# A hybrid attention and convolution layer: the convolution's state outputs written by DMA with exchanged dimensions instead of transposed on TensorE

## The chip, the cores and the metric

The kernel runs on one core of one Trainium2 chip. The metric is the device time of one execution in microseconds (us). The kernel before took 470.9 us, the median of three runs (470.34 to 470.97).

## The reference

One layer of a streaming encoder for two requests that share the weights: a prompt of 1024 frames and a running stream of 64 frames, both of model width 1024, with 16 meta tokens. One input projection gives q, k, v, an attention gate, a GLU pair and a convolution gate. Group A is sliding-window attention, group B a depthwise convolution of width 31; both are normalised, gated and go through a shared output projection.

```
a, b = jnp.split(glu, 2, axis=-1)
u = a * jax.nn.sigmoid(b)
...
conv = _conv_branch(u, left, conv_w, ln_g, ln_b, w_pw)
...
new_conv_prompt = u[:, -(CONV_W - 1):]                                   # (30, 512)
new_conv_sample = concatenate([state_conv, us], axis=1)[:, -(CONV_W-1):] # (30, 512)
```

The last two lines, shortened here, are the outputs that the change touches: the last 30 rows of the convolution's input, for the prompt and for the running stream, with 512 channels in a row.

## The kernel before

All 1104 tokens go through the input projection feature-major: a weight tile of 128 output features (`w_in[m]`, 128 x 1024, loaded into `wraw`) is split into two float32r parts, `whi` and `wlo`, and three products, hi·hi, hi·lo and lo·hi, make up a float32 product on TensorE. `unit(mi, n, done)` gives the 24 products of weight tile `mi` and token chunk `n` (384, 384 and 336 or 320 tokens) as a list of closures; `fill(k)` runs the next k of them from a queue, `drain()` all that are left, so the order of TensorE's work is written out by hand. `WORDER` is the order of the weight tiles: 20 is the keys, 21 the values, 4 to 7 and 8 to 11 the GLU pair, 0 to 3 the queries, 12 to 19 the gates.

`ahead` runs the weights' pipeline. In the first unit of a tile it issues the load of the tile after next (`load_raw`, line 184, on SyncE's queue, two `wraw` buffers). In a later unit it splits the next tile: `whi` on ScalarE, and `wlo` on VectorE or by a copy of -whi on ScalarE and an accumulating DMA of `wraw` from GpSimd's queue. For the GLU tiles, `wlo` is made half by the one and half by the other. A `wraw` buffer is free for the next load when both are done.

The GLU units write `u{i}` for i = 0 to 3: 128 channels on the partitions, and along the row 30 state columns, 1024 prompt columns, 30 state columns and 64 sample columns (`UW` in all). Its last piece is written by VectorE in `glu`, after which the 31 taps of the convolution over `u{i}` (`conv`) go on a list. VectorE works through the taps between its other duties: `tick` issues taps as long as the time given to VectorE is less than that given to TensorE plus `AHEAD`, counted in the table `given` by fixed prices. `mm` and `tp` add the prices of TensorE's work.

`conv_outs(i)` writes the state outputs of 128 channels. The columns `SEQ` to `SEQ + LEFT` of `u{i}` are the last 30 prompt frames, the last 30 columns those of the running stream. Both are transposed on TensorE into one PSUM tile (`uo{i}`, line 108), copied by ScalarE into `uso{i}`, and written by two DMAs of 30 rows x 512 B (lines 479 and 480). Its four calls stand among the units: for u0 after the first key unit, for u1 in the middle of the last key unit, for u2 in the last value unit and for u3 in the last unit of the first query tile.

Matmuls, ScalarE, VectorE and GpSimd instructions keep the order in which the program gives them. SyncE's DMAs in this stage are placed by the tile framework's scheduler, which knows what each of them waits for, and stay in that order on the queue.

Of the kernel before, what the change touches and what calls it, by code (L numbers as in the profile page):

```python
# [10 lines left out]
F32 = mybir.dt.float32  # L11
F32R = mybir.dt.float32r
AF = mybir.ActivationFunctionType
ALU = mybir.AluOpType

P = 128
D = 1024
SEQ = 1024
# [8 lines left out]
LEFT = W - 1  # L27
UW = LEFT + SEQ + LEFT + DEC
# [20 lines left out]
def layer_kernel(ctx: ExitStack, tc: tile.TileContext, x, x_fm, w_in, w_pw, w_out, vec, g_post,  # L49
                 bias_in, cache_kT, cache_k, cache_v, stateT,  # L50
                 y_p, y_s, nk_p, nv_p, nc_p, nk_s, nv_s, nc_s):
    nc = tc.nc
# [40 lines left out]
    act, dve, pool = Engine(nc.scalar, "act", 200, 0.82), Engine(nc.vector, "dve", 60, 1.18), Engine(nc.gpsimd)  # L93
# [12 lines left out]
    def tp(*a, **k):  # L106
        given["pe"] += 109
        return tc.keep_in_program_order(nc.tensor.transpose(*a, **k))  # L108
# [5 lines left out]
    sm = ctx.enter_context(tc.tile_pool(name="sm", bufs=2))  # L114
    psum = ctx.enter_context(tc.tile_pool(name="psum", bufs=1, space=bass.MemoryType.PSUM))

    def ps_tile(tag, bufs, name):
        return psum.tile([P, 512], F32, tag=tag, bufs=bufs, name=name)
# [14 lines left out]
    def any_ps(i, name):  # L133
        return ps_tile(*(("mm", 3), ("s", 2), ("pt", 2))[i % 3], name)

    def slot(tag, name, shape=(P, 1152), dt=F32):
        return m4.tile(list(shape), dt, tag=tag, bufs=4 if tag == "B" else 2, name=name)
# [3 lines left out]
    ident = const.tile([P, P], F32, name="ident")  # L141
# [329 lines left out]

    def conv_outs(i):
        u = us[i]
        ps = ps_tile("pt", 2, f"uo{i}")
        tp(ps[:LEFT, 0:P], u[:, SEQ:SEQ + LEFT], ident)
        tp(ps[:LEFT, P:2 * P], u[:, UW - LEFT:UW], ident)
        so = sm.tile([P, 2 * P], F32, tag="gate", bufs=7, name=f"uso{i}")
        act.activation(so[:LEFT], ps[:LEFT, :2 * P], AF.Copy)
        nc.sync.dma_start(nc_p[:, i * P:(i + 1) * P], so[:LEFT, 0:P])
        nc.sync.dma_start(nc_s[:, i * P:(i + 1) * P], so[:LEFT, P:2 * P])  # L480

    def conv(i):
        u = us[i]
# [420 lines left out]
    add_kv(KM, kTb)  # L904
    fill(24)
    conv_outs(0)
    fill(36)
    conv_outs(1)
    drain()
    add_ab(2)  # L910
    drain()
    vfm = slot("T", "vfm")
    add_kv(VM, vfm)
    fill(60)
    conv_outs(2)
    drain()
    add_ab(3)
    fill(24)
    kxy = split_keys()
    for g in range(3):  # L920
        ps = ps_tile("pt", 2, f"vt{g}")
# [13 lines left out]
    so = slot("P", "kvo", (P, 2 * P))  # L935
# [22 lines left out]
    i = -1  # L958
    while (i := i + 1) < max(len(order) + 2, L0 + 7 if L0 < 99 else 0):
# [9 lines left out]
        if 3 <= i < len(order) + 3:  # L969
            c = order[i - 3]  # L970
# [18 lines left out]
        if n == 0:  # L989
            while taps:  # L990
                f, j = taps.pop(0)
# [138 lines left out]
    for T in (0, 1, 8, 2, 3, 4, 5, 6, 7):  # L1130
# [12 lines left out]
        for j, (j0, j1) in enumerate(zip(cuts, cuts[1:])):  # L1143
            js = slice(j0, j1)
            for half in (1, 0):
                ps = any_ps(ny := ny + 1, f"y{T}_{j}_{half}")[:, :j1 - j0]
# [23 lines left out]
        o = slot("P", f"o{T}", (P, D))  # L1170
# [79 lines left out]
```

## Time and profile before

| | |
|---|---|
| median of three runs | 470.9 us (470.34 to 470.97) |
| the profiled execution | 470.69 us |
| its span in the profile | 468.9 us |
| granted clock of TensorE, mean over the span | 0.997 |
| TensorE busy (matmul) | 456.2 us, 97% |
| VectorE busy | 380.1 us, 81% |
| ScalarE busy | 231.3 us, 49% |
| GpSimd busy | 75.0 us, 16% |
| packets on SyncE's DMA queue | 14584, 37.31 MB |

The profiled execution lies 0.2 us below the median of the runs, and 1.8 us of its time are outside the span. PE is TensorE, PEld its weight loads, DVE VectorE, ACT ScalarE, POOL GpSimd; SPq and POOLq are the sequencers of SyncE and GpSimd, which issue DMAs. In the profile most operations of ScalarE, VectorE and GpSimd have line 86, where a helper records them, and all matmuls line 104, so they are told apart by their tiles; the profile leaves the numbers of tiles out (`u` for `u0`, `out_dram` for every output). The input projections before the attention reach from the start to about 187 us; the four calls of `conv_outs` lie at 64, 70, 106 and 144 us.

### The profile page before, as it was taken

Reading aid. Unit: us, or ns where it says so; the run is one execution under the profiler, and the core shown is the slowest. Engines: PE = TensorE matmul, PEld = TensorE weight load, DVE = VectorE, ACT = ScalarE, POOL = GpSimd, SP = SyncE. Lnnn points to the kernel's source line nnn. Section 1 sums busy time; section 2 is a strip of 40 time slices with the busy share of each in tenths; the row PEclk is TensorE's granted clock in tenths of the full one; section 3 lists DMA queues with packets and bytes.
Section 4 is the critical chain, followed back from the end, with each engine's and each line's share of the span. In section 5 each row is a group of like instructions: output and inputs, shape, how many; then the busy total and the mean of one; then the engine's idle time right before and its main releaser. Section 6 shows DMA issues by size and latency. Waiting matters only on the chain.

```text
span 468.9 us, 7427 instructions
## 1 busy us (share of the span) xinstructions
PE 456.2 (97%) x2809; PEld 416.7 (89%) x2809; DVE 380.1 (81%) x672; ACT 231.3 (49%) x534; POOL 75.0 (16%) x106
## 2 busy tenths in 40 slices
PE   7999999999999999999999999999999999999994
PEld 6999999999999999998988988797899787888884
DVE  3669999999999999999899987996999547554443
ACT  6585532135032223666766856774977335333322
POOL 0000100013000000010111113254024411111100
PEclk9999999999999999999999999999999999999998
DMA  8992144035023333330101010111252212222231
GB/s 271 402 344 117 36 105 126 0 86 153 13 68 93 89 91 91 89 94 5 48 7 49 6 52 4 48 55 42 97 175 90 91 67 91 67 92 90 97 124 48
DMA packets 16491, 43.54 MB, mean 93 GB/s; under 512 B 2600, under 2 KB 4888, under 8 KB 16456
## 3 DMA queue, kind: packets, MB, share of 16 engines
q1 hardware_dynamic: 14584, 37.31, 23.4%
q0 software_dynamic: 1872, 5.77, 6.6%
q8 instruction: 22, 0.36, 0.3%
q14 instruction: 13, 0.11, 0.1%
HBM read 32.00 MB, written 4.84 MB: 79 GB/s over the span
## 4 chain that ended last, share of the span: by engine, by line
PE 85%; DVE 8%; DMA 2%; ACT 2%; issue 1%; POOL 1%; SPq 0%; DVEq 0%; POOLq 0%; ACTq 0%
PE g L104 53%; PE y L104 20%; PE av L104 3%; PE s L104 3%; DVE wo L86 2%; DVE H L86 2%; PE pa L108 2%; PE pb L108 1%; DMA x<-in_x_fm_dram 1%; DMA woraw<-in_w_out_dram 1%; DVE wlo L86 1%; POOL sqc L86 1%; DVE qb L86 1%; DVE zl L86 1%; DVE sqc L86 0%
## 5 line engine op out<-in xcount | busy, mean ns | idle before, releaser
L104 PE MATMUL g<-xT,whi 128*128 128x384 f32 (+2 forms) x960 | 222.8, 332 | 1.1 <-ACT xT L86 0.9
L104 PEld LDWEIGHTS g<-xT,whi 128*128 128x128 f32 x960 | 168.3, 188 | 8.5 <-issue 5.4
L86 DVE SCALAR_TENSOR_TENSOR H<-u,vec_t,H 128x1118 f32<-128x1118 f32 x120 | 166.6, 1388 | 3.2
L104 PE MATMUL g<-xT,wlo 128*128 128x384 f32 (+2 forms) x480 | 139.1, 332 | 0.5 <-DVE wlo L86 0.5
L104 PEld LDWEIGHTS g<-xT,wlo 128*128 128x128 f32 x480 | 88.0, 188 | 2.7 <-issue 1.2
L104 PE MATMUL y<-wo,mh 128*128 128x512 f32 (+2 forms) x304 | 89.2, 381 | 0.0
L104 PEld LDWEIGHTS y<-wo,mh 128*128 128x128 f32 (+1 forms) x304 | 55.2, 185 | 11.5
L104 PE MATMUL y<-wo,ml 128*128 128x512 f32 (+1 forms) x136 | 51.3, 379 | 0.1
L86 DVE SCALAR_TENSOR_TENSOR y<-y,small,y 128x512 f32<-128x512 f32 (+1 forms) x19 | 13.7, 721 | 31.2 <-PE y L104 29.6
L86 ACT ACTIVATE T<-T,st 128x210 f32<-128x210 f32 (+2 forms) x84 | 36.6, 450 | 4.2 <-DVE st L86 4.1
L86 POOL DMA_DIRECT2D wlo<-wraw x13 | 11.5, 885 | 148.8 <-ACT wlo L86 112.9
L104 PEld LDWEIGHTS y<-wo,ml 128*128 128x128 f32 x136 | 25.6, 188 | 4.8 <-DVE ml L86 0.4
L86 ACT ACTIVATE yj<-y 128x512 f32<-128x512 f32 (+2 forms) x21 | 12.8, 609 | 31.8 <-DVE y L86 31.7
L86 ACT ACTIVATE whi<-wraw 128x1024 fp32r<-128x1024 f32 (+1 forms) x23 | 22.4, 978 | 6.3 <-PE g L104 6.1
L104 PE MATMUL g<-xT,wq 128*128 128x384 f32 (+1 forms) x144 | 25.4, 333 | 0.0
L104 PEld LDWEIGHTS g<-xT,wq 128*128 128x128 f32 x144 | 24.2, 188 | 0.5
L86 ACT ACTIVATE sg<-g 128x384 f32<-128x384 f32 (+1 forms) x10 | 4.7, 473 | 37.1 <-PE g L104 37.1
L86 ACT ACTIVATE qb<-g 128x384 f32<-128x384 f32 (+1 forms) x12 | 5.7, 474 | 32.1 <-PE g L104 32.1
L86 DVE CUSTOM_DVE_ANT_0 T<-s,bias 128x210 f32<-128x210 f32 (+2 forms) x68 | 20.6, 359 | 0.8 <-PE s L104 0.8
L86 ACT ACTIVATE y<-y,small 128x512 f32<-128x512 f32 (+1 forms) x19 | 12.6, 666 | 16.7 <-PE y L104 16.6
L86 POOL TENSOR_TENSOR asq<-asq 128x128 f32<-128x128 f32 (+2 forms) x18 | 12.7, 707 | 38.5 <-ACT asq L86 37.8
L86 ACT ACTIVATE qb<-av 128x256 f32<-128x256 f32 x17 | 6.4, 379 | 23.6 <-PE av L104 23.6
(199 smaller groups left out, 611.3 us busy)
## 6 DMA issues: line engine op xcount, KB each, us to landing
wraw<-in_w_in_dram SPq DMA_DIRECT2D x18, 512.0 KB, 3.4
wlo<-wraw POOLq DMA_DIRECT2D x9, 512.0 KB, 4.6
H<-in_x_dram SPq DMA_DIRECT2D x8, 512.0 KB, 8.2
xr<-in_x_dram SPq DMA_DIRECT2D x8, 512.0 KB, 4.0
out_dram<-o SPq DMA_DIRECT2D x7, 512.0 KB, 2.9
woraw<-in_w_out_dram SPq DMA_DIRECT2D x5, 512.0 KB, 3.3
wraw<-in_w_in_dram SPq DMA_DIRECT2D x8, 256.0 KB, 5.6
x<-in_x_fm_dram SPq DMA_DIRECT2D x4, 384.0 KB, 5.9
```

Of the source, the lines that this page charges most:

```text
L86: ins = op(*a, **k)
L104: return tc.keep_in_program_order(nc.tensor.matmul(out, lhsT=lhsT, rhs=rhs, **k))
L108: return tc.keep_in_program_order(nc.tensor.transpose(*a, **k))
```

## The change

The transpositions, the PSUM tile, the ScalarE copy and the tile `uso` go. The two DMAs read `u{i}` as it stands, 128 partitions x 30 elements, and write the output with its two dimensions exchanged, so that neighbouring elements of a partition land 2048 B apart:

```diff
     def conv_outs(i):
         u = us[i]
-        ps = ps_tile("pt", 2, f"uo{i}")
-        tp(ps[:LEFT, 0:P], u[:, SEQ:SEQ + LEFT], ident)
-        tp(ps[:LEFT, P:2 * P], u[:, UW - LEFT:UW], ident)
-        so = sm.tile([P, 2 * P], F32, tag="gate", bufs=7, name=f"uso{i}")
-        act.activation(so[:LEFT], ps[:LEFT, :2 * P], AF.Copy)
-        nc.sync.dma_start(nc_p[:, i * P:(i + 1) * P], so[:LEFT, 0:P])
-        nc.sync.dma_start(nc_s[:, i * P:(i + 1) * P], so[:LEFT, P:2 * P])
+        for out, o in ((nc_p, SEQ), (nc_s, UW - LEFT)):
+            nc.sync.dma_start(out[:, i * P:(i + 1) * P].rearrange("s c -> c s"), u[:, o:o + LEFT])
```

The change moves the outputs on SyncE's queue. Before, from the key cache `kc` on (`out_4` and `out_7` are the two state outputs, `wraw10` and `wraw21` are weight tiles, the number after a name is a running one):

```order
L835 DMA kc_633<-in_cache_kT_dram 128x128
L184 DMA wraw10_643<-in_w_in_dram 128x1024
L837 DMA vcache_635<-in_cache_v_dram 128x128
L838 DMA out_5_dram<-in_cache_k_dram 16x512
L839 DMA out_6_dram<-in_cache_v_dram 16x512
L479 DMA out_4_dram<-uso0_675 30x128
L480 DMA out_7_dram<-uso0_675 30x128
L184 DMA wraw21_750<-in_w_in_dram 128x1024
L479 DMA out_4_dram<-uso1_731 30x128
L480 DMA out_7_dram<-uso1_731 30x128
L184 DMA wraw7_789<-in_w_in_dram 128x1024
```

The same stretch of SyncE's queue in the changed kernel:

```order
L830 DMA kc_633<-in_cache_kT_dram 128x128
L475 DMA out_4_dram<-u0_187 128x30x1
L475 DMA out_7_dram<-u0_187 128x30x1
L184 DMA wraw10_643<-in_w_in_dram 128x1024
L832 DMA vcache_635<-in_cache_v_dram 128x128
L833 DMA out_5_dram<-in_cache_k_dram 16x512
L834 DMA out_6_dram<-in_cache_v_dram 16x512
L475 DMA out_4_dram<-u1_281 128x30x1
L475 DMA out_7_dram<-u1_281 128x30x1
L184 DMA wraw21_740<-in_w_in_dram 128x1024
```

Each pair of outputs now stands one weight load earlier: that of u0 ahead of wraw10, that of u1 ahead of wraw21. Further on, the pair of u2 stands between wraw11 and wraw0 (before, between wraw0 and wraw1), and that of u3 between wraw2 and wraw3 (before, between wraw3 and wraw16).

Without the prices of `tp` and of the copies, the taps fall a little differently among VectorE's work. VectorE before, from the first wlo10 half on (`H` is the convolution's output, one row with x3 is three taps):

```order
L86 TENSOR_TENSOR wlo10_753<-wraw10_643,whi10_752 128x512
L86 SCALAR_TENSOR_TENSOR H_89<-u0_187,vec_t_84,H_89 128x1118 x3
L86 MEMSET u2_785 128x14
L86 SCALAR_TENSOR_TENSOR H_89<-u0_187,vec_t_84,H_89 128x1118 x3
L86 TENSOR_TENSOR u2_785<-g6_0_749,sg2_0_818 128x384
L86 SCALAR_TENSOR_TENSOR H_89<-u0_187,vec_t_84,H_89 128x1118 x5
L86 TENSOR_TENSOR u2_785<-g6_1_821,sg2_1_876 128x384
```

The same stretch of VectorE in the changed kernel:

```order
L86 TENSOR_TENSOR wlo10_743<-wraw10_643,whi10_742 128x512
L86 SCALAR_TENSOR_TENSOR H_89<-u0_187,vec_t_84,H_89 128x1118 x2
L86 MEMSET u2_774 128x14
L86 SCALAR_TENSOR_TENSOR H_89<-u0_187,vec_t_84,H_89 128x1118 x3
L86 TENSOR_TENSOR u2_774<-g6_0_739,sg2_0_807 128x384
L86 SCALAR_TENSOR_TENSOR H_89<-u0_187,vec_t_84,H_89 128x1118 x6
L86 TENSOR_TENSOR u2_774<-g6_1_810,sg2_1_866 128x384
```

One tap has moved from ahead of the first piece of u2 to behind it; the number of taps is the same. The order of TensorE's, ScalarE's and GpSimd's other instructions is as before.

## Rows read from the trace of the kernel before

**Rows 1.** The page: the span, the engines' busy time, the chain that ended last by engine

```profile
span 468.9 us, 7427 instructions
PE 456.2 (97%) x2809; PEld 416.7 (89%) x2809; DVE 380.1 (81%) x672; ACT 231.3 (49%) x534; POOL 75.0 (16%) x106
PE 85%; DVE 8%; DMA 2%; ACT 2%; issue 1%; POOL 1%; SPq 0%; DVEq 0%; POOLq 0%; ACTq 0%
```

**Rows 2.** Waits of TensorE, whole span, longest first: total us, times, longest us

```profile
PE warm_ps L104 <- POOL rx L86: 1.4, 1, 1.4
```

**Rows 3.** Busy time by stretch: us, then PE, PEld, DVE, ACT, POOL, clock, DMA

```profile
340.00:360.00 20.00, 18.78 (x141) 18.10 (x141) 19.48 (x27) 15.73 (x29) 7.42 (x7) 1.00 0.48 154
```

**Rows 4.** Timeline of TensorE around the first pair: start us, us, instruction

```profile
63.59 0.38 PE L108 MATMUL uo<-ident,u 128*30 128x128 f32 x2
...
64.16 0.34 PE L104 MATMUL g<-xT,wlo 128*128 128x384 f32 x1
...
64.68 0.33 PE L104 MATMUL g<-xT,wlo 128*128 128x384 f32 x1
```

**Rows 5.** The page's costliest groups: the convolution's taps (busy us, mean ns)

```profile
L86 DVE SCALAR_TENSOR_TENSOR H<-u,vec_t,H 128x1118 f32<-128x1118 f32 x120 | 166.6, 1388 | 3.2
```

**Rows 6.** DMA, 97.7 to 102.9 us, one weight load: packets, MB, share; us to landing

```profile
q1 hardware_dynamic: 144, 0.52, 27.5%
issues: line engine op xcount, KB each, median us to landing
wraw<-in_w_in_dram SPq DMA_DIRECT2D x1, 512.0 KB, 3.1
```

**Rows 7.** DMA, 80.6 to 81.4 us, the end of a state load

```profile
q1 hardware_dynamic: 49, 0.00, 4.6%
```

**Rows 8.** DMA, 64.4 to 67 us, the two old outputs of u0

```profile
q1 hardware_dynamic: 90, 0.03, 5.4%
...
out_dram<-uso SPq DMA_DIRECT2D x2, 15.0 KB, 1.4
```

**Rows 9.** DMA, 66.5 to 71.45 us, an accumulating DMA of GpSimd's queue

```profile
q0 software_dynamic: 144, 0.52, 55.9%
```

**Rows 10.** Timeline of VectorE: the last pieces of u0 and u1

```profile
53.68 0.62 DVE L86 TENSOR_TENSOR u<-g,sg 128x256 f32<-128x256 f32 x3
...
60.74 0.63 DVE L86 TENSOR_TENSOR u<-g,sg 128x256 f32<-128x256 f32 x3
```

**Rows 11.** Timeline of SyncE's queue: wraw10, wraw21, wraw0, wraw2

```profile
59.72 0.33 SPq L184 DMA_DIRECT2D wraw<-in_w_in_dram  x1
...
71.50 0.37 SPq L184 DMA_DIRECT2D wraw<-in_w_in_dram  x1
...
107.85 0.33 SPq L184 DMA_DIRECT2D wraw<-in_w_in_dram  x1
...
135.62 10.46 SPq L184 DMA_DIRECT2D wraw<-in_w_in_dram  x2
```

**Rows 12.** The page's DMA issues: GpSimd's half loads (KB each, us to landing)

```profile
wlo<-wraw POOLq DMA_DIRECT2D x4, 256.0 KB, 3.3
```

**Rows 13.** Timeline of ScalarE: whi10, whi21, whi0, whi3

```profile
72.43 1.05 ACT L86 ACTIVATE whi<-wraw 128x1024 fp32r<-128x1024 f32 x1
...
92.26 1.06 ACT L86 ACTIVATE whi<-wraw 128x1024 fp32r<-128x1024 f32 x1 [3.05 <-PE g L104]
...
130.29 1.06 ACT L86 ACTIVATE whi<-wraw 128x1024 fp32r<-128x1024 f32 x1 [3.05 <-PE g L104]
...
162.70 1.05 ACT L86 ACTIVATE whi<-wraw 128x1024 fp32r<-128x1024 f32 x1
```

**Rows 14.** Timeline of GpSimd: the DMAs of half wlo10 and half wlo21

```profile
74.44 0.87 POOL L86 DMA_DIRECT2D wlo<-wraw  x1 [6.69 <-ACT wlo L86]
94.28 0.87 POOL L86 DMA_DIRECT2D wlo<-wraw  x1 [18.97 <-ACT wlo L86]
```

**Rows 15.** Timeline of TensorE: the first products with wlo10 and wlo21

```profile
78.82 1.37 PE L104 MATMUL g<-xT,wlo 128*128 128x384 f32 x7
...
98.68 1.55 PE L104 MATMUL g<-xT,wlo 128*128 128x384 f32 x8
```

## The prediction

> **What bounds the kernel now.** Read the page first: TensorE is busy for 97% of the span, VectorE for 81% and ScalarE for 49%, and 85% of the chain that ended last is TensorE [rows 1]. The waits of TensorE come second: its longest wait in the whole span is 1.4 us [rows 2]. So in the projections, where the change is, a nanosecond of TensorE is a nanosecond of the span, as long as its weights arrive. VectorE comes close behind: in the stretch 340 to 360 us it is the busier one, 19.48 of 20 us against 18.78 [rows 3]. Third, the timelines of SyncE, ScalarE and GpSimd around the four calls of `conv_outs` show how much room the weight loads have, and fourth, the packets of single transfers show what a small packet costs.
>
> **What goes away.** Eight transpositions, in four pairs. Around the first pair, 0.57 us pass from its start at 63.59 to the wlo product at 64.16, for the pair and two whi products; three products at the regular step take 64.68 - 64.16 = 0.52, so 0.173 each [rows 4]. The pair costs 0.57 - 2 x 0.173 = 0.22 us; four pairs, 0.9 us, all on the path. Four ScalarE copies (out of PSUM) go too; they are hidden, since the copy's successors wait for TensorE anyway and ScalarE is half idle [rows 1]. Their cover gone would only make ScalarE earlier, so I take nothing.
>
> **What moves.** The recording layer counts TensorE's time, and so the convolution's taps shift by one place among VectorE's other work. Their number is unchanged. A tap takes 1.39 us [rows 5], so one instruction that TensorE waits for may come that much earlier or later; the tap moves behind it at some places and ahead of it at others, so I take zero, with half a microsecond either way in the forecast's own range.
>
> **What is added.** Eight DMAs of 128 partitions x 30 elements, each element going to its own place in DRAM: 3840 pieces of 4 bytes. A load of 128 rows has 144 packets [rows 6], that is 128 + 16, so it runs on 16 engines with one closing packet each; one output then puts 240 + 1 packets on every engine. The price of a 4-byte packet is in no row. Call p its time and X = 241 p the time of one output.
> - From below: the last 49 packets of a state load, all under 512 B, took 4.6% of 16 engines for 0.8 us, 12 ns each [rows 7]. X = 2.9 us.
> - The old state outputs, the same data in 512 B rows to the same DRAM: 90 packets in 5.4% of 16 x 2.6 us, 25 ns each [rows 8]. X = 6.0 us.
> - From above: an accumulating DMA, which reads its target and writes it back, took 55.9% of 16 x 4.95 us for 144 packets, 307 ns each [rows 9]; a plain load 27.5% of 16 x 5.2 us, 159 ns [rows 6]. If every 4-byte piece paid that whole extra of 148 ns over 12 ns, X = 38.6 us.
>
> I take 25 ns, the row with the same direction and target, so X = 6.0. The Trainium skill, VectorE: DVE Perf Modes, The three transpose paths, speaks against such a change: a plain strided transposition by DMA is 19 times slower than the crossbar's 1309 ns for 128 x 128. By that an estimate for our 3840 elements is 5.8 us per output, so the sum would stay as it is; no run here shows that figure.
>
> **Where the added time lies.** Issuing one is cheap, but SyncE's transfers queue behind each other on the same engines. In the new order the pair of u0 stands ahead of the load wraw10, the pair of u1 ahead of wraw21, and the pair of u3 ahead of wraw3. The old outputs waited for the transposition and stood behind wraw10.
>
> u0 is complete on VectorE at 53.68 + 0.62 = 54.3 [rows 10]. A small output needed 1.4 us from issue to landing [rows 8], so the pair runs from about 55.7 to 55.7 + 2X. wraw10, issued at 59.72 as before [rows 11], lands behind it, about 2.4 us later (a free load takes 3.1 us from issue [rows 6], of which I count 0.7 as overlapped): 58.1 + 2X. ScalarE splits wraw10 at 72.43 [rows 13]. Half of wlo10 then goes through GpSimd's DMA at 74.44 [rows 14] and lands 3.3 us later [rows 12] at 77.7; TensorE uses it at 78.82 [rows 15]: 1.1 us of room. Two removed pairs of transpositions bring that use forward by 0.45. So the deadline is 72.43 + 1.1 - 0.45 = 73.1, and TensorE loses 2X - 15.0 if that is positive: nothing up to **X = 7.5 us, or 31 ns per packet**. At X = 6.0 wraw10 lands at 70.1, with 3 us to spare.
>
> The pair of u1 (complete at 60.74 + 0.63 [rows 10]) follows wraw10 and three small copies, for which I allow 0.5: it ends at 58.6 + 4X, and wraw21 lands at 61.0 + 4X, now issued no earlier than 71.50 [rows 11]. Its deadline by the same steps is 92.26 [rows 13] + 1.1 (GpSimd at 94.28, landing 97.6, use at 98.68 [rows 14, 15]) - 0.45 = 92.9, plus what was lost before. It adds 2X - 16.9, so nothing up to X = 8.5. The u2 pair follows wraw11 and has only wraw0 behind it in a hurry, which was issued at 107.85 [rows 11] and is needed at 130.29 [rows 13]: a pair that starts with u2, at about 100, leaves room for X up to about 14. The u3 pair is behind wraw2 (issued at 135.62 [rows 11], landing at 138.7); wraw3 lands at 141.1 + 2X and is needed at 162.70 [rows 13], so X up to 10.8 even without the room that its second half leaves. GpSimd's own DMAs share the engines: nine of their packets per engine, each letting one small packet pass, lose 9 x 25 ns = 0.2 us of their 1.1 us.
>
> **The sum.** At X = 6.0 all eight outputs are hidden and 0.9 us of TensorE's work is gone. The profiled execution took 470.69 us, so 469.8 by it; it stands 0.2 us below the median of the runs, 470.9, so against the median **470.0 us**. About 0.2%, 0.94 us, is what a measurement of this kernel can tell from no change; the forecast is close to that edge. Its own range is 469.3 to 470.6.
>
> **Rivals.**
> 1. *VectorE keeps the time.* TensorE arrives 0.9 us earlier and waits for VectorE in the layer norm and the split of z. For it: VectorE is the fuller engine from 340 to 360 us [rows 3]. Against: it is only 8% of the chain [rows 1], and follows TensorE's results before. Time: 470.9, between 470.6 and 471.4.
> 2. *The weights come late.* The two pairs ahead of wraw10 and wraw21 pass their deadline: slower. It decides at p = 31 ns, between the 25 ns taken and twice that. At 50 ns, X = 12.0: wraw10 costs 24 - 15.0 = 9.0, wraw21 24 - 16.9 = 7.1, wraw3 lands 165.1 - 162.7 = 2.4 late, which I take to be within the room of its second half. 470.0 + 16.1 = 486.1. At 38 ns (all time of [rows 8] put on its 60 data packets) X = 9.2, the loss is 3.4 + 1.5, the time 474.9.
> 3. *Each piece is a read-modify-write* that the engine or the memory serves one at a time, p over 50 ns. The far end, X = 38.6, costs 62.2 at wraw10 and 60.3 at wraw21 alone: 592 us or more. The Trainium skill, DMA: Bandwidth & Descriptors, Specifications, states that transfers below 512 B do a read-modify-write; the trace before has no write to DRAM that small, so no run here shows it yet.
>
> **How the numbers follow.** The rows stand on both sides of 31 ns, but two of the three nearest prices are below. I give the forecast 0.42, rival 1 0.17, rival 2 0.25 and rival 3 0.16. Faster by over 0.2% is 0.6 of the forecast's chance, 0.25. Same is the rest of the forecast (0.17), most of rival 1 (0.15) and the edge of rival 2 just past 31 ns (0.03): 0.35. Slower is 0.40. The range runs from 469.3, the lower end of the forecast, to 486.1, the 50 ns end of rival 2; it leaves out rival 3 (0.16) and about 0.04 below.
>
> **What the profile after would show.** No uo and uso rows, and about 30,700 more small packets on SyncE's queue. The time to landing of the first output gives X; two of them back to back, under 15 us together, is the forecast. Right: whi10 on ScalarE at about 72, with no wait for wraw. Wrong: ScalarE, then VectorE and TensorE wait for wraw10 just after 72 us, and again for wraw21 after 92 (rivals 2 and 3), or there is no such wait and TensorE's waits for VectorE after 310 us have grown by 0.9 us (rival 1). A pair of 60 us or more says rival 3.

## The result, and the profile after

The changed kernel took **633.22 us**, the median of three runs (629.17 to 636.8), against 470.9 us before: 1.3447 times the time, with a 95% interval from 1.3401 to 1.3494. The forecast was 470.0 us, and the range ended at 486.1. The profiled execution took 636.8 us.

The page of the changed kernel, for [rows 1]: the span, the engines' busy time, TensorE's granted clock in 40 slices, SyncE's DMA queue, and the chain that ended last by engine and by line.

```profile
span 635.0 us, 7407 instructions
PE 466.8 (74%) x2801; PEld 425.6 (67%) x2801; DVE 380.8 (60%) x672; ACT 230.1 (36%) x530; POOL 75.7 (12%) x106
...
PEclk9999555957798559975599999999999999999998
...
q1 hardware_dynamic: 45072, 37.31, 54.4%
...
PE 52%; DMA 26%; issue 11%; DVE 7%; ACT 2%; POOL 1%; SPq 0%; DVEq 0%; POOLq 0%; ACTq 0%
```

The span has grown by 166.1 us. TensorE's idle time went from 468.9 - 456.2 = 12.7 to 635.0 - 466.8 = 168.2 us, which is 155.5 of it; the other 10.6 us are busy time of TensorE, although it has eight instructions fewer. The growth lies before 318 us, where the weights of the projections arrive; the bytes on the queue are the same, the packets 30,488 more.

The windows of the changed kernel around three of the long waits (columns as in [rows 3]):

```profile
53.80:107.00 53.20, 8.24 (x52) 7.92 (x50) 18.30 (x22) 1.01 (x2) 1.43 (x3) 0.60 1.30 10
...
134.00:144.00 10.00, 0.02 (x1) 0.02 (x1) 7.54 (x7) 1.19 (x2) 0.87 (x1) 0.50 1.50 21
...
266.00:313.00 47.00, 8.24 (x50) 7.92 (x50) 42.72 (x32) 0.93 (x2) 0.87 (x1) 0.64 1.67 12
```

From 134 to 144 us TensorE stands, and the granted clock is 0.50, its lower level of 1.2 GHz; 0.60 and 0.64 are means over stretches in which it worked for 8.2 us and then stood. So the products that follow a wait begin at the lower level: the first eight at 108.31 us take 2.93 us, shown below, where eight took 1.55 before [rows 15]. That is how busy time grows without more instructions.

The waits of TensorE in the changed kernel, for [rows 2]: us in total, times, longest.

```profile
PE g L104 <- DMA wlo<-wraw: 156.2, 5, 46.3
PE warm_ps L104 <- POOL rx L86: 1.4, 1, 1.4
```

Five waits make up 156.2 of the 166.1 us. They are for `wlo<-wraw`, the accumulating DMAs of GpSimd's queue, which move data from one on-chip tile to another. The timelines of the changed kernel, of SyncE, GpSimd, ScalarE and TensorE in this order, for [rows 11, 13, 14]: start, duration, instruction, idle time before it and what ended it.

```profile
53.78 2.43 SPq L475 DMA_DIRECT2D out_dram<-u  x2
108.33 0.35 SPq L184 DMA_DIRECT2D wraw<-in_w_in_dram  x1
...
110.59 30.84 SPq L475 DMA_DIRECT2D out_dram<-u  x2
...
54.67 1.05 POOL L86 DMA_DIRECT2D wlo<-wraw  x1 [15.82 <-ACT wlo L86]
114.11 0.87 POOL L86 DMA_DIRECT2D wlo<-wraw  x1 [58.01 <-ACT wlo L86]
135.52 0.87 POOL L86 DMA_DIRECT2D wlo<-wraw  x1 [20.54 <-ACT wlo L86]
...
133.51 1.06 ACT L86 ACTIVATE whi<-wraw 128x1024 fp32r<-128x1024 f32 x1 [13.59 <-DMA wraw<-in_w_in_dram]
...
108.31 2.93 PE L104 MATMUL g<-xT,wlo 128*128 128x384 f32 x8 [46.27 <-DMA wlo<-wraw]
143.98 2.93 PE L104 MATMUL g<-xT,wlo 128*128 128x384 f32 x8 [21.77 <-DMA wlo<-wraw]
162.55 1.65 PE L104 MATMUL g<-xT,wlo 128*128 128x384 f32 x4 [10.97 <-DMA wlo<-wraw]
```

The two outputs of u0 are issued from 53.8 us on. The accumulating DMA of wlo20 is issued 0.9 us later and lands 53.6 us after its issue, where 4.6 is the median; TensorE stands for 46.3 us until 108.3. The load wraw10, issued at 59.72 before [rows 11], is issued at 108.33 here and used at 133.51, not at 72.43 [rows 13]. It is late because it takes the buffer of wraw20, which wlo20's accumulating DMA still reads. SyncE's waits for such DMAs show this, the first line in the changed kernel, where the longest, of 52.0 us, ends with that issue, the second in the one before:

```profile
SPq L184 <- DMA wlo<-wraw: 228.8, 12, 52.0
...
SPq L184 <- DMA wlo<-wraw: 153.3, 13, 23.7
```

The next waits of TensorE are for wlo6 (issued at 114.11, landing after 29.8 us) and for half of wlo10 (135.52, after 27.0). The eight outputs land, pair by pair, after 48.7 and 78.7 us, 50.0 and 60.8, 32.9 and 49.5, 38.2 and 53.1. The DMA of wlo20 lands 6 us after the first output of u0 (102.5) and 25 us before the second, so it is not held up until the whole pair is done.

At first the engines take the packets fast. DMA packets of the changed kernel in the first 3 us of the pair (53 to 56 us), for [rows 8]:

```profile
q1 hardware_dynamic: 2053, 0.01, 31.3%
```

That is 31.3% of 16 x 3 us for 2053 packets, 7 ns each, below the lowest bound of the prediction. But ten microseconds a little later (70 to 80 us), for [rows 9], look like this:

```profile
q0 software_dynamic: 44, 0.18, 109.1%
q1 hardware_dynamic: 141, 0.00, 59.8%
```

A small packet now takes 680 ns, and a packet of the accumulating DMA 4 us in place of 0.31 [rows 9]. The pieces start fast, and then the transfers on these engines crawl; what slows them, the isolated transfers below show.

### The profile page after: what moved, and what is told of

It reads as the page before. It is cut to its first block, busy times and chain, and to the rows that moved or that the text cites. A ratio compares the mean times of both kernels' runs of the same rounds, so it can differ in the third digit from the quotient of the medians.

```text
span 635.0 us, 7407 instructions
## 1 busy us (share of the span) xinstructions
PE 466.8 (74%) x2801; PEld 425.6 (67%) x2801; DVE 380.8 (60%) x672; ACT 230.1 (36%) x530; POOL 75.7 (12%) x106
## 3 DMA queue, kind: packets, MB, share of 16 engines
q1 hardware_dynamic: 45072, 37.31, 54.4%
## 4 chain that ended last, share of the span: by engine, by line
PE 52%; DMA 26%; issue 11%; DVE 7%; ACT 2%; POOL 1%; SPq 0%; DVEq 0%; POOLq 0%; ACTq 0%
PE g L104 28%; DMA wlo<-wraw 19%; PE y L104 15%; DMA wraw<-in_w_in_dram 5%; PE av L104 2%; DVE H L86 2%; PE s L104 2%; DVE wo L86 1%; PE pa L108 1%; PE pb L108 1%; DMA x<-in_x_fm_dram 1%; DMA woraw<-in_w_out_dram 1%; DVE wlo L86 1%; POOL sqc L86 0%; DVE qb L86 0%
## 5 line engine op out<-in xcount | busy, mean ns | idle before, releaser
L104 PE MATMUL g<-xT,wlo 128*128 128x384 f32 (+2 forms) x480 | 146.2, 350 | 156.7 <-DMA wlo<-wraw 156.2
L104 PE MATMUL g<-xT,whi 128*128 128x384 f32 (+2 forms) x960 | 225.3, 335 | 0.2 <-DVE xT L86 0.2
L104 PEld LDWEIGHTS g<-xT,wlo 128*128 128x128 f32 x480 | 93.1, 200 | 160.6 <-DMA wlo<-wraw 157.8
L104 PEld LDWEIGHTS g<-xT,whi 128*128 128x128 f32 x960 | 171.7, 191 | 7.6 <-issue 5.4
L86 DVE TENSOR_TENSOR wlo<-wraw,whi 128x512 fp32r<-128x512 f32 (+1 forms) x14 | 12.7, 912 | 64.6 <-ACT whi L86 64.6
L86 DVE TENSOR_TENSOR u<-g,sg 128x384 f32<-128x384 f32 (+3 forms) x20 | 6.9, 382 | 62.5 <-ACT sg L86 62.4
L86 DVE TENSOR_TENSOR qs<-qb,qs 128x256 fp32r<-128x256 f32 x17 | 9.1, 536 | 46.1 <-ACT qs L86 46.1
L86 ACT ACTIVATE whi<-wraw 128x1024 fp32r<-128x1024 f32 (+1 forms) x23 | 22.4, 978 | 21.6 <-DMA wraw<-in_w_in_dram 18.6
L86 ACT ACTIVATE kTb<-g 128x384 f32<-128x384 f32 (+1 forms) x3 | 1.4, 479 | 56.7 <-PE g L104 56.7
```

The costliest lines, as they stand in the source:

```text
L86: ins = op(*a, **k)
L104: return tc.keep_in_program_order(nc.tensor.matmul(out, lhsT=lhsT, rhs=rhs, **k))
```

## The experiments

**What a piece costs, by itself.** At the end of the kernel before, when all its work is done, isolated transfers:

```diff
+    def exchanged(out, i):
+        keep(nc.sync.dma_start(out[:, i * P:(i + 1) * P].rearrange("s c -> c s"), st[:, 0:LEFT]))
...
+    settle()
+    exchanged(nc_p, 0)
+    settle()
...
```

`settle()` writes the tiles of the transfers anew, which has to wait until the transfer ahead has landed; the cuts are marked.

> The kernel before with a tail behind its last output: eight small tests, each started only when the one ahead has landed. (1) one output with exchanged dimensions, 3840 pieces of 4 bytes to places 2048 B apart; (2) as many 4-byte pieces, to neighbouring places of the same output; (3) as many pieces into on-chip memory; (4) the same 15 KB as 128 rows of 120 B; (5) a pair of exchanged outputs beside one accumulating DMA of 512 KB from GpSimd's queue; (6) a pair beside a plain 512 KB load from GpSimd's queue; (7) that accumulating DMA alone; (8) that load alone. The tail overwrites the state outputs with zeros in another layout. Theory A, the pieces are dear by themselves: after a first burst of some 2000 they go at 130 per us, whatever runs beside them; then (1) takes about 16 us, (5) and (6) 40 to 50 us. Theory B, the pieces are cheap (7 to 9 ns each on 16 engines, as in the first burst) and get dear only beside GpSimd's accumulating DMA: (1) takes about 4 us, (6) about 6 us, and only (5) 40 us or more. If the spread places are the cause, (2) is much faster than (1); if the writes to DRAM are, (3) is about 4 us and (2) like (1); if the count of pieces on the engines is, (3) is as slow as (1). (4) about 2.5 us, (7) 4.6 and (8) 3.4 under every theory.

From issue to landing: one exchanged output alone 50.0 us; the same number of 4-byte pieces to neighbouring places in DRAM 26.8; the same number into on-chip memory 4.0; as 128 rows of 120 B 1.6. A pair beside an accumulating DMA: 52.4 and 80.5, the accumulating DMA 57.8. A pair beside a plain 512 KB load from GpSimd's queue: 43.2 and 60.2, the load 31.9. The accumulating DMA and the load without a pair, which ran beside each other, took 5.5 and 6.2, more than the 4.6 and 3.4 expected. The packets of the first test, in the DMA view of this kernel from 469 to 490 us:

```profile
q1 hardware_dynamic: 3856, 0.02, 39.8%
...
out_dram<-st_src SPq DMA_DIRECT2D x1, 15.0 KB, 50.0
```

All 3856 packets of the output, which was issued at 469.42, are recorded by 490 us, and none from 490 to 520; yet VectorE, which waits for the landing, goes on only then:

```profile
519.52 0.11 DVE L86 MEMSET st_src<- 128x60 f32 x1 [50.12 <-DMA out_dram<-st_src]
```

So some 30 us pass between the last recorded packet and the landing. The profile does not show what fills them; writes that still drain into DRAM fit, since the same number of packets with an on-chip target land after 4.0 us. 3840 writes of 4 bytes into DRAM cost 50 us, 13 ns each on average. The theory that such an output is cheap alone falls, and so does the 16 us that I had expected for it from the burst at its start. Neighbouring places take about half (26.8), so both the target and the spread count.

**Reads, fewer pieces, denser places.** The same kind of tail, with other transfers:

> The kernel before with seven isolated transfers added at its end, which overwrite some state outputs with zeros; only their times from issue to landing count. (1) 3840 pieces of 4 bytes READ from DRAM with exchanged dimensions (4096 B steps) into on-chip memory; (2) an exchanged write with 15 of the 30 frames; (3) one with 64 of the 128 channels; (4) an exchanged write into one dense stretch of 15 KB (steps of 512 B in place of 2048); (5) 3840 on-chip pieces beside an accumulating 512 KB DMA; (6) the reads of (1) beside it; (7) one exchanged write beside it. Theory D, a write of a piece into DRAM is what is slow (the memory has to merge it into something wider) and the small packet is not: (1) under 10 us, (2) and (3) about 25 us, half of 50, (5) and (6) with the accumulating DMA under 12 us, (7) about 50 us. Theory E, any access of 4 bytes to DRAM is slow: (1) near 50 us, (6) held up to 30 us or more. Theory F, small packets of any kind keep the engines from the other queue: (5) held up too, over 15 us. For (4): near the 27 us of neighbouring pieces if the distance in DRAM decides; near 50 us if it is that neighbours are written by different engines.

| transfer | us to landing |
|---|---|
| 3840 pieces of 4 bytes read from DRAM, exchanged | 10.5 |
| exchanged write, 15 of 30 frames | 27.2 |
| exchanged write, 64 of 128 channels | 37.0 |
| exchanged write into a dense 15 KB | 16.4 |
| on-chip pieces; the accumulating DMA beside them | 6.7; 6.1 |
| exchanged reads; the accumulating DMA beside them | 10.5; 12.0 |
| one exchanged write; the accumulating DMA beside it | 47.1; 47.3 |

Theory D comes nearest: the direction decides most, 10.5 us to read where a write takes 50.0. Its figures were not all met: it had the reads under 10, the accumulating DMA beside them under 12, and half the channels at 25. Theories E and F fall. The DMA view of this kernel around the last test (583 to 585 us) and around the test with the reads (568 to 570 us):

```profile
acc_dst<-big_src POOLq DMA_DIRECT2D x1, 512.0 KB, 47.3
out_dram<-st_src SPq DMA_DIRECT2D x1, 15.0 KB, 47.1
...
acc_dst<-big_src POOLq DMA_DIRECT2D x1, 512.0 KB, 12.0
st_dst<-in_x_dram SPq DMA_DIRECT2D x1, 15.0 KB, 10.5
```

The accumulating DMA lands about with the pieces in both cases, though its source and its target are on-chip tiles. What it shares with them are the DMA engines, and its packets of 4 us in the view above show it held up there. It need not last as long as the pieces: beside a pair it landed after 57.8 us, between the two outputs, and the plain load after 31.9, ahead of both. Where the pieces go counts too: the dense target (steps of 512 B) takes a third of the steps of 2048 B, though neighbours come from different partitions there as well. Neither of the two figures expected for it (27 and 50 us) came. Half the channels cost more than half; why, these numbers don't tell.

**Small rows in the same place.** The outputs as they lie, 128 rows of 120 B, at the same place of the queue:

```diff
-            nc.sync.dma_start(out[:, i * P:(i + 1) * P].rearrange("s c -> c s"), u[:, o:o + LEFT])
+            flat = out.rearrange("s c -> (s c)")[i * LEFT * P:(i + 1) * LEFT * P]
+            nc.sync.dma_start(flat.rearrange("(c s) -> c s", s=LEFT), u[:, o:o + LEFT])
```

> The changed kernel with each state output written as 128 rows of 120 B, one per channel, at the same place on SyncE's queue: the output's dimensions are not exchanged, so its values stand in another order. Nothing else differs. If the pieces are the cause (theories A and B), all of the loss goes, and what is left is the gain of the removed transpositions: 470.9 - 0.9 = 470.0 us, or 470.9 if VectorE keeps it. If the new place on SyncE's queue, ahead of the weight loads, is the cause (theory C), it stays far slower than before.

470.4 us against 470.85, ratio 0.9985, interval 0.9976 to 0.9994. The place on the queue, ahead of wraw10 and wraw21, costs nothing that shows; the whole loss goes with the exchange.

**Half the pieces.** Only the prompt's outputs exchanged, those of the running stream as rows of 120 B:

> The changed kernel with only the prompt's outputs in exchanged dimensions; the stream's outputs go as 128 rows of 120 B, their dimensions not exchanged. Half the pieces. Under theory A the first 2000 pieces or so of each call are absorbed at once and only the other 1800 wait at 130 per us: each call takes about 16 us instead of about 50, and TensorE's wait for wlo falls by far more than half, from 156 us to 30 to 60; time 500 to 530 us. Under theory B, or if the time goes with the pieces from the first one on, it falls by half, to 78 us or so, time about 550 us.

605.45 us in the fastest of four runs (the others 615.2 to 622.58), so at least 134.6 us of the 162.3 are still lost. In the profiled execution, of 617.47 us, the four exchanged outputs land after 51.6, 51.4, 43.2 and 32.9 us, and TensorE's waits for `wlo<-wraw` are 139.3 us in four. I had expected the loss to fall much further, under both theories. A second output behind the first adds only some 30 us (80.5 after 52.4 in the isolated pair), and in the changed kernel the first long wait ended 6 us after the first output of its pair had landed. So most of a pair's cost comes with its first output. Why two drain partly side by side stays open.

**One pair.** Only the outputs of u3 exchanged:

```diff
+            if i == 3:
                 nc.sync.dma_start(out[:, i * P:(i + 1) * P].rearrange("s c -> c s"), u[:, o:o + LEFT])
+            else:
+                flat = out.rearrange("s c -> (s c)")[i * LEFT * P:(i + 1) * LEFT * P]
+                nc.sync.dma_start(flat.rearrange("(c s) -> c s", s=LEFT), u[:, o:o + LEFT])
```

> The changed kernel with only the outputs of u3 exchanged; those of u0 to u2 go out as 128 rows of 120 B, not exchanged. If each pair costs by itself what the stall behind it showed (TensorE busy 8.2 of 47 us from 266 to 313 us, so some 39 us lost): 505 to 515 us. If the loss of the changed kernel comes from pairs that pile up behind one another: under 490 us.

519.03 us against 471.15, so 47.9 us for one pair, a little over what I had expected, and one wait in TensorE's list:

```profile
PE g L104 <- DMA wlo<-wraw: 46.8, 1, 46.8
```

Four pairs cost 162.3 us together, 40.6 each, so the loss comes from each pair by itself; nothing has to pile up.

**Without accumulating DMAs.** Every wlo by VectorE, in the changed kernel and, as a control, in the one before:

```diff
-        if p > 3 and not on_dve and freer() == "act":
-            act.activation(lo, hi.bitcast(F32), AF.Copy, scale=-1.0)
-            pool.dma_start(out=lo, in_=raw, accum_op=ALU.add)
-            return
```

> The changed kernel, with every wlo made by VectorE, so no accumulating DMA is left that the pieces could hold up; the weight loads still stand behind the pieces on SyncE's queue. Theory G, the held-up accumulating DMAs carry nearly all of the 162 us: under 520 us. Theory H, either path alone is enough, since the loads lie behind the same slow pieces (wraw10 landed at 133 us where TensorE needs it at about 73, so 60 us for u0, then 25 us for each later pair by what its load is late): 560 to 620 us, with TensorE waiting for whi or VectorE's wlo, that is for wraw.

> Control for the run without accumulating DMAs: the kernel before with every wlo made by VectorE. Both theories: VectorE has some ten subtractions more, 1.1 us or so each, and it is the nearly full engine, so 470 to 485 us.

634.42 us, and 485.62 for the control: 148.8 us lost, where theory G had under 520 us in all. Both times lie a little above the ranges that theory H gave, 560 to 620 and 470 to 485. The waits of TensorE and of ScalarE in the changed kernel without accumulating DMAs:

```profile
PE g L104 <- ACT whi L86: 110.5, 4, 47.3
...
ACT whi L86 <- DMA wraw<-in_w_in_dram: 139.7, 4, 46.1
```

Theory H holds: the pieces block two paths. Where the accumulating DMAs are gone, ScalarE waits four times, once for each pair, for a weight load that stands behind the pieces on SyncE's queue: wraw10, issued right behind the pair of u0 at 56.85 us, lands after 66.0 us. That the other path is enough as well, the first wait of the changed kernel shows: whi20 was made at 52.21, before the pair was issued, so only wlo20's DMA was missing. The wait for wlo hides most of the loads' delay there; ScalarE waits only 18.6 us for `wraw`.

**One transposition instead of two.** The kernel before, with the 124 columns from `SEQ` on transposed at once:

```diff
-        tp(ps[:LEFT, 0:P], u[:, SEQ:SEQ + LEFT], ident)
-        tp(ps[:LEFT, P:2 * P], u[:, UW - LEFT:UW], ident)
+        n = UW - SEQ
+        tp(ps[:n, 0:P], u[:, SEQ:UW], ident)
...
```

> The kernel before with one transposition per call instead of two: the 60 wanted columns of u lie within 124 neighbouring ones, which one transposition takes together; ScalarE copies 124 x 128 instead of 30 x 256. The whole computation is done. Four transpositions less, 0.11 us each by the pair's 0.22: 0.45 us less, 470.4 us, by every theory; a difference that can hardly be told from none.

470.41 us against 470.85, ratio 0.999, interval 0.9981 to 0.9999. Four of eight transpositions give 0.44 us, half of the 0.9 that the prediction put on eight; the interval reaches from 0.05 to 0.9 us.

**The exchange on the reading side.** Since reads of pieces took a fifth of the time of writes:

```diff
-            nc.sync.dma_start(out[:, i * P:(i + 1) * P].rearrange("s c -> c s"), u[:, o:o + LEFT])
+            raw = nc.dram_tensor(f"raw{i}_{o}", (P, LEFT), F32, kind="Internal").ap()
+            nc.sync.dma_start(raw, u[:, o:o + LEFT])
+            so = sm.tile([LEFT, P], F32, tag="gate", bufs=7, name=f"uso{i}_{o}")
+            nc.sync.dma_start(so, raw.rearrange("c s -> s c"))
+            nc.sync.dma_start(out[:, i * P:(i + 1) * P], so)
```

> The changed kernel with the exchange on the reading side: each output is written to a stretch of DRAM as 128 rows of 120 B, read back with exchanged dimensions in pieces of 4 bytes into 30 rows of an on-chip tile, and written out as 30 rows of 512 B. No transposition on TensorE, and the outputs are those of the reference. By the isolated transfers an output costs 1.6 us to write, 10.5 us to read and 1.4 to 2.8 us to write again, some 15 us instead of 50, and an accumulating DMA beside the reads takes 12.0 us instead of 5.5. If that is hidden: 470.0 to 470.5 us, as without exchange. If the 6.5 us that an accumulating DMA is late lie past the 1.1 us of room of wlo10 and wlo21, or a weight load waits on SyncE's queue behind a read that waits for its write: 475 to 490 us. Were 4-byte pieces slow in any direction, over 550 us.

**469.87 us** against 470.69 (469.07 to 470.86 in ten runs), ratio 0.9982, interval 0.9972 to 0.9991: 0.8 us faster than the kernel before, and far faster than the changed one. Its page, with SyncE's queue, and the DMA issues from 60 to 120 us:

```profile
span 468.1 us, 7434 instructions
...
q1 hardware_dynamic: 46576, 37.55, 27.8%
```

```profile
wraw<-in_w_in_dram SPq DMA_DIRECT2D x6, 512.0 KB, 3.5
wlo<-wraw POOLq DMA_DIRECT2D x2, 512.0 KB, 5.5
wlo<-wraw POOLq DMA_DIRECT2D x3, 256.0 KB, 4.2
uso<-raw SPq DMA_DIRECT2D x6, 15.0 KB, 5.7
```

It has more packets on SyncE's queue than the changed kernel, 46,576 against 45,072, as many 4-byte pieces among them, on the same queue and in the same stretch of the program. But a read of 3840 pieces lands after 5.7 us (median of six; here its pieces lie 120 B apart in DRAM, in the isolated read 4096 B). The accumulating DMAs land after 5.5 and 4.2 us instead of 4.6 and 3.3 [rows 12], and TensorE's longest wait is again the 1.4 us at the start. In the stretch from 54 to 80 us of this kernel (the columns are those of [rows 3]) TensorE never stops:

```profile
54.00:80.00 26.00, 26.00 (x158) 26.00 (x157) 25.28 (x30) 6.26 (x9) 3.17 (x5) 1.00 0.72 83
```

## Why the prediction was wrong, step by step

**What bounds the kernel, what goes away, what moves: right.** Eight transpositions were put at 0.9 us, a ratio of 0.9981. The run with small rows (0.9985) and the one with reads (0.9982) hold it within their intervals, and half of the transpositions gave half of it, though within a wide interval. So VectorE did not keep the time, and rival 1 falls: it would have shown in these runs. The moved taps cost nothing that these runs show.

**The price of a piece: wrong, and this step decided.** "I take 25 ns, the row with the same direction and target, so X = 6.0." X was 50.0 us, eight times that, and over the upper bound of 38.6 too. The row had the direction and the target, but 512 B to a packet, and a price per packet was carried from it to 4-byte packets as if the engine's time were the price. The packets took 7 ns on the engine at first; what counted was the DRAM side, on average 13 ns for each of 3840 writes, where on-chip memory took all of them in 4.0 us. Both bounds were taken from what packets take on the engines, so neither could hold it. The Trainium skill, VectorE: DVE Perf Modes, The three transpose paths, warns of this kind of change, a plain copy that transposes by its steps, with a large step in its destination. By its factor of 19 on 1309 ns, a figure for bf16, the estimate for an output was 5.8 us; the 50.0 measured is almost nine times that, and the measurement decides. That such a copy is the slow way agrees.

**The pieces and GpSimd's DMAs: wrong.** "Nine of their packets per engine, each letting one small packet pass, lose 9 x 25 ns = 0.2 us of their 1.1 us." They lost some 49 us at wlo20, and five such waits make up 156.2 of the 166.1 us. Sharing the engines did not mean letting one packet pass in turn: a packet of the accumulating DMA took 4 us in place of 0.31.

**The deadlines: near in number, by another path.** With 78.7 us for 2X the prediction's landing of wraw10 is 58.1 + 78.7 = 136.8, a loss of 63.7; whi10 started at 133.51, 3.3 earlier. Half of wlo10 then took 27.0 us on GpSimd's queue instead of 3.3, 23.7 more. Together 63.7 - 3.3 + 23.7 = 84.1; the first product with wlo10 came at 162.55 instead of 78.82 [rows 15], 83.7 late. That these agree so well is in part luck. The prediction had wraw10 issued at 59.72 and waiting behind the pair; here it was not issued before 108.33, when wlo20's DMA had freed its buffer, and landed 25.2 us later. The first to stop TensorE was wlo20, from 62 us on, then wlo6, and the prediction had seen neither at risk. The run without accumulating DMAs shows the path that the formula had in mind.

**The rivals.** Rival 3 (0.16) had the price on its side: its sign, a pair of 60 us or more, came with 78.7, and its time of 592 us or more with 633. But it got there by late weight loads alone, the path of the run without accumulating DMAs, where the changed kernel waits for wlo; so in its time, too, there is some luck. It had the pieces served one at a time by "the engine or the memory". The runs point behind the engine, since on-chip pieces take 4.0 us and the landing comes some 30 us after the last packet; whether it is the memory itself or the way to it, they do not part. The Trainium skill, DMA: Bandwidth & Descriptors, Specifications, names a read-modify-write below 512 B; that the reads took 10.5 us where the writes took 50.0 agrees with it, but 128 rows of 120 B, also below that size, took 1.6 us, so here the number of writes mattered far more than being below it. That each write is in fact a read and a write of something wider is an explanation that fits, and was not shown. Rival 2's range ended at 50 ns a packet; per engine and packet it was 207 (50.0 us over 241).

## What to carry to other kernels

Price a rearranging DMA by the number of its writes into DRAM and by where they go, not by its bytes or by a row of larger packets: 3840 elements of 4 bytes with 2048 B between them take 50 us, into a dense 15 KB 16.4. Transfers that share the engines with them, on-chip ones of another queue too, come late by tens of microseconds. If an exchange of dimensions is to be done by DMA, put it on the side that is read, and write whole rows; here that gave 469.87 us. Where a price stands in no row, a bound from rows of another packet size is no bound: let the range reach the rival that it would exclude.

## What the runs showed of the hardware

- 3840 pieces of 4 bytes: 4.0 us into on-chip memory, 10.5 us read from DRAM, 16.4 us written into a dense 15 KB, 26.8 us as neighbouring pieces of one partition's row, 50.0 us with steps of 2048 B.
- The packets of an output are all recorded by 490 us and it lands at 519.5: a DMA queue can look idle in the packet view while its transfer has yet to land.
- An accumulating DMA of 512 KB between on-chip tiles takes 47.3 to 57.8 us beside such writes, 12.0 beside the reads, 6.1 beside on-chip pieces and 5.5 beside a plain load; a 512 KB load from the same queue takes 31.9 beside the writes and 6.2 without.
- The instruction that issues the second output of u1 kept SyncE for 24.0 us, from 117.43 on; what stands behind it on the queue is issued only after that.
- While TensorE stood from 134 to 144 us its granted clock was 0.50, 1.2 GHz, and eight products that followed such a wait took 2.93 us in place of 1.55; its busy time over the span grew by 10.6 us.
